# A hybrid decoder layer on one Trainium2 core: weight units of 1024 columns instead of 512

## The chip, the cores and the metric

The kernel runs on one core of one Trainium2 chip. The metric is the device time of one execution in microseconds (us), the lower the better. Of the kernel before there are three timed runs and one profiled execution.

## What is computed

One step of a decoder layer for 1024 new prompt tokens and 32 sample tokens (8 sequences of 4), model width 1024, all in fp32:

```python
proj = x @ w_in                                  # q, k, v, GLA's q, k, v, gates
o_a  = dilated_window_attention(...)             # 3 groups x 8 heads, windows 128, 512, 2048
o_b  = gla_recurrence(...)                       # 4 heads, chunks of 64
x1   = layer_norm(alpha * x + merge(o_a, o_b, gates) @ w_out)
q    = normalise(x1 @ w_peer_query)              # 8 heads
expert, gate = top 16 of 128 x 128 product keys  # per token and head
act  = gelu(x1 . u_table[expert])                # one neuron per expert, 16384 experts
y    = layer_norm(alpha * x1 + sum(gate * act * v_table[expert]))
```

The outputs are y for both groups, the new key and value buffers (for the samples the old ones, shifted) and the new GLA states.

## The kernel before

**fp32 products.** Each fp32 matmul is done as three: operands are split into a high part (a rounded copy, by ScalarE) and a low part (source minus high, by VectorE), and `mm3` (lines 186 to 189) adds high times high, low times high and high times low into one PSUM bank. `split_into` (lines 158 to 160) makes the two parts; the copy is recorded at line 145, in `copy_act`, and the subtraction at line 160.

**Weights.** They are streamed through SBUF. `load_w_` (lines 173 to 184) takes a staging buffer `wst` (three of 2 KB per partition), has SP load 128 x 512 values into it at line 174, takes `wh` and `wl` (four buffers each) and splits. `load_w` calls it at an earlier priority than the code around it. While there are output copies left (old key and value buffers that go from DRAM to DRAM, in the list `copies`), a counter `due` sends one or two of them behind a load, at line 180. All loads, copies and gate reloads are issued by SP, in one order. A staging buffer is free again when VectorE has made the low part from it.

**Stages.** The first 1000 us of the span are projections. From 1000 to 2700 us there are attention, GLA, the merge, the PEER queries and top-k, and gathers begin. From 2700 us on the dense PEER loop runs beside the rest of the gathers. The 1024 prompt tokens are treated in two ways: for one half the experts of each token are gathered (`peer_gather`, line 1217: GpSimd, in the trace POOL, issues one indirect DMA of 128 rows of 1024 values per expert slot, at line 1234 for `pu` and at line 1255 for `pv`; VectorE multiplies and adds up, at lines 1240 and 1273, with four `gr` buffers), for the other half (512 tokens) all 16384 experts are computed densely.

**The dense loop** (`peer_dense`, line 1354) goes over 128 values of e, each standing for 128 experts. For an e there are four pieces of work:

- `hidden(e)`: the uT weights in two units of 512 columns, 24 matmuls into one PSUM bank (`ps<-pg,wh` in the trace), then a gelu on ScalarE at line 1380 into a `t` or `tb` tile;
- `weights(e)`: VectorE multiplies that tile by the gate matrix G (line 1388, two instructions, one for each half of G), then it is split into a pair of `tq`;
- `values(e)`: two loads from `pv` into `wst` at line 1374, split into the two halves of a page `pg`;
- `out`: 18 matmuls for output columns 0 to 5, into PSUM banks that stay open over the whole loop; for each pair of e another 12 for columns 6 and 7, into two `ps` banks that VectorE adds to a sum at line 1423.

`hidden` runs up to seven e ahead. G stands in DRAM; every eight e, line 1407 loads the next eight into two pages (2 transfers of 1 MB). This makes 16 reloads. Pages are one pool of ten, shared by G, the `pv` pairs and the activations of the 512 tokens; the pages for a new G come free when TensorE has done columns 6 and 7 of an earlier pair.

**The order.** A scheduler, which has a simulated timeline of its own, lays the instructions of each engine in one list before the kernel is built. On the chip each engine goes through its list in that order; an instruction that must wait holds up all that is behind it on that engine.

Of the kernel before, what the change touches and what calls it, by code (L numbers as in the profile page):

```python
# [11 lines left out]
F32R = mybir.dt.float32r  # L12
# [9 lines left out]
P = 128  # L22
T = 512
NS = 32
TW = T + NS
D = 1024
# [57 lines left out]
def tile_hybrid_step(ctx, tc, I, O, dbg=None):  # L84
# [31 lines left out]
    def sb(shape, tag, bufs, dt=F32):  # L116
        return sp.tile(list(shape), dt, tag=tag, bufs=bufs, name=nm(tag))
# [5 lines left out]
        return sb(shape, "t2", 8, dt)  # L123

    def tb(shape, dt=F32):
        return sb(shape, "tb", 9, dt)

    def tq(shape, dt=F32):
        return sb(shape, "tq", 6, dt)
# [40 lines left out]
        return r  # L170

    def load_w_(src, shape):
        st = sb(shape, "wst", 3)
        ld = nc.sync.dma_start(st, src)
        due[0] += CRATE
        for _ in range(2):
            if copies and not hush[0] and due[0] >= 1:
                due[0] -= 1
                with tc.issue_after(ld.ins):
                    nc.sync.dma_start(*copies.pop(0))  # L180
        hi = sb(shape, "wh", 4, F32R)
        lo = sb(shape, "wl", 4, F32R)
        split_into(st, hi, lo)
        return hi, lo

# [58 lines left out]
    def tick():  # L244
        for l in lanes.values():
            l[2] += l[1]
            while l[2] >= 1:
                l[2] -= 1
                step(l)
# [249 lines left out]
    def rows_of(toks, src, xs, cols=None, stag=0):  # L499

        outs = [(ps() if i < 4 else (pb if busy[0] else pc)())[:m] for i, m in toks]
        def products(p_, i, m, k, w):
            if i < 4 and cols:
                h, l = [cols(v, i) for v in xs(k, 0, T)]
            else:
                h, l = xs(k, i * P, i * P + m)
            mm3(p_, h, l, *w, k == 0, k == 7)


        for k in range(8):  # L510
            tick()
            if k <= 8 - stag:
                ws = []
            ws.append(load_w(src[:, k], [P, 512]))
            if k < 8 - stag:
                for p_, (i, m) in zip(outs, toks):
                    products(p_, i, m, k, ws[0])
        for p_, (i, m) in zip(outs, toks):
            for j in range(stag):
                products(p_, i, m, 8 - stag + j, ws[j])  # L520
        return outs


    def phase_a(b):
# [18 lines left out]
        def dense_T(src, nk, xs, width=P):  # L543

            out = [(ps(), c0, c1) for (c0, c1) in (segs0 if xs is x else segs)]
            for k0 in range(0, nk, 4):
                wh, wl = load_w(src[:, k0:k0 + 4], [P, 4, width])
                for k in range(k0, k0 + 4):
                    for (p_, c0, c1) in out:
                        h, l = xs(k, c0, c1)  # L550
                        mm3(p_[:width, :c1 - c0], wh[:, k - k0], wl[:, k - k0], h, l, k == 0, k == nk - 1)
            return out

        def proj_T(ci):
# [799 lines left out]
    def peer_dense(x1T, toks):  # L1354
# [4 lines left out]

        def hidden(e):  # L1360
            p_ = ps()
            for k0 in (0, 4):
                wh, wl = load_w(I["uT"][e][:, k0:k0 + 4], [P, 4, P])
                for k in range(4):
                    h, l = x1T(k0 + k, 0, T)
                    mm3(p_, wh[:, k], wl[:, k], h, l, k0 + k == 0, k0 + k == 7)
            return p_

        def values(e):
            v = page([P, 2, D], F32R)  # L1370
            for hf in range(2):
                st = sb([P, 512], "wst", 3)
                c = slice(hf * 512, (hf + 1) * 512)
                nc.sync.dma_start(st, vrows[e][:, c])
                split_into(st, v[:, 0, c], v[:, 1, c])
            return v

        def gelu(e):
# [351 lines left out]
```

## Time and profile before

| what | us |
|---|---|
| timed runs | 4253.96, 4259.05, 4264.85; median 4259.05 |
| profiled execution, its own time | 4250.62 |
| its span, from the first to the last instruction | 4248.5 |
| TensorE busy | 3842.8 (90%) |
| VectorE busy | 3089.3 (73%) |
| ScalarE busy | 1522.4 (36%) |
| GpSimd (POOL) busy | 1324.2 (31%) |

PE is TensorE, DVE VectorE, ACT ScalarE, POOL GpSimd; SP issues DMAs and is not counted as busy. The mean granted clock of TensorE is 0.911 of its full one. Tile names in the profile have no numbers: `ps<-pg,wh` is a matmul into a `ps` bank from an activation page and a high weight part, `wl<-wst,wh` the making of a low part. `A <- B` in a wait means that A waited and that B ended the wait. In the profile 2.1 us of the execution lie outside the span.

### The profile page before, as it was taken

What the parts mean: (1) busy time and instruction counts of PE and PEld (TensorE: products, weight loads), DVE (VectorE), ACT (ScalarE), POOL (GpSimd) and SP (SyncE); (2) the same over time, 40 slices, a digit from 0 to 9 for tenths busy, and PEclk for the clock granted to TensorE, in tenths of its full rate; (3) what the DMA queues carried; (4) which work ended last, traced back from release to release, by engine and by line L of the source; (5) the groups of instructions that cost most, each with busy time, mean ns of one, the idle gap of its engine ahead of it and who ended that gap; (6) DMA issues with size and microseconds to landing.
All of it is one profiled execution on the core that took longest, in us unless ns stands there. A gap on an engine that the chain in (4) does not pass through costs nothing.

```text
span 4248.5 us, 55341 instructions
## 1 busy us (share of the span) xinstructions
PE 3842.8 (90%) x18338; PEld 2908.0 (68%) x18338; DVE 3089.3 (73%) x6887; ACT 1522.4 (36%) x3092; POOL 1324.2 (31%) x1163
## 2 busy tenths in 40 slices
PE   8999999999796789899779977789999999999997
PEld 7898676656685467656667634577777777777776
DVE  2334432548999866688988877898887887888887
ACT  3334222335443344422234447442222233322223
POOL 0000000000345333344544142315444443444441
PEclk9999999999997579779989975799999999999998
DMA  8665565877798778778988466868899898998986
GB/s 270 196 216 191 191 206 169 298 269 247 253 312 278 243 253 277 238 237 293 318 302 277 159 224 236 277 203 288 312 311 313 294 314 300 319 311 303 312 305 217
DMA packets 455158, 1118.36 MB, mean 263 GB/s; under 512 B 48484, under 2 KB 133620, under 8 KB 444486
## 3 DMA queue, kind: packets, MB, share of 16 engines
q0 software_dynamic: 156672, 570.49, 39.4%
q1 hardware_dynamic: 298198, 544.32, 38.6%
q8 instruction: 144, 2.36, 0.2%
q14 instruction: 144, 1.18, 0.1%
HBM read 1044.14 MB, written 158.37 MB: 283 GB/s over the span
## 4 chain that ended last, share of the span: by engine, by line
PE 47%; DMA 16%; issue 14%; DVE 13%; POOL 6%; ACT 4%; SPq 0%; POOLq 0%; DVEq 0%; ACTq 0%
PE ps L187 10%; PE ps L188 10%; PE ps L189 9%; POOL gr L1234 5%; DMA gr<-pv,tkei 5%; DMA pg<-Gd 4%; DMA gr<-pu,tkei 3%; DVE gr L1240 3%; DVE acc L1273 2%; PE pc L1335 1%; DVE wl L160 1%; PE pb L358 1%; DMA wst<-uT 1%; PE pc L1336 1%; POOL gr L1255 1%
## 5 line engine op out<-in xcount | busy, mean ns | idle before, releaser
L187 PE MATMUL ps<-pg,wh 128*128 128x512 f32 (+3 forms) x2488 | 898.9, 363 | 72.3 <-ACT wh L145 52.1
L1255 POOL DMA_INDIRECT gr<-pv,tkei x544 | 662.9, 1219 | 966.3 <-DVE acc L1273 633.8
L1234 POOL DMA_INDIRECT gr<-pu,tkei x544 | 642.3, 1181 | 965.2 <-DVE gr L1240 561.2
L188 PE MATMUL ps<-pg,wl 128*128 128x512 f32 (+3 forms) x2488 | 896.1, 361 | 10.5 <-DVE wl L160 10.5
L189 PE MATMUL ps<-pg,wh 128*128 128x512 f32 (+3 forms) x2488 | 893.9, 360 | 0.0
L145 ACT ACTIVATE wh<-wst 128x512 fp32r<-128x512 f32 x740 | 462.9, 628 | 1183.5 <-DMA wst<-uT 384.4
L160 DVE TENSOR_TENSOR wl<-wst,wh 128x512 fp32r<-128x512 f32 x740 | 502.2, 683 | 375.6 <-ACT wh L145 347.6
L1240 DVE SCALAR_TENSOR_TENSOR gr<-gr,x1g 128x1024 f32<-128x1024 f32 x544 | 659.1, 1218 | 101.3 <-DMA gr<-pu,tkei 99.7
L1273 DVE SCALAR_TENSOR_TENSOR acc<-gr,act,acc 128x1024 f32<-128x1024 f32 x512 | 654.4, 1278 | 82.6 <-DMA gr<-pv,tkei 80.1
L187 PEld LDWEIGHTS ps<-pg,wh 128*128 128x128 f32 (+1 forms) x2488 | 472.9, 190 | 168.4 <-ACT wh L145 57.2
L188 PEld LDWEIGHTS ps<-pg,wl 128*128 128x128 f32 (+1 forms) x2488 | 473.3, 190 | 95.6 <-DVE wl L160 16.7
L189 PEld LDWEIGHTS ps<-pg,wh 128*128 128x128 f32 (+1 forms) x2488 | 472.9, 190 | 77.3 <-issue 10.4
L187 PE MATMUL ps<-wh,pg 128*128 128x512 f32 x832 | 342.2, 417 | 38.3 <-ACT wh L145 18.9
L188 PE MATMUL ps<-wh,pg 128*128 128x512 f32 x832 | 341.0, 410 | 3.6 <-DVE pg L160 3.6
L189 PE MATMUL ps<-wl,pg 128*128 128x512 f32 x832 | 322.3, 414 | 2.1 <-DVE wl L160 1.9
L145 ACT ACTIVATE pg<-wst 128x512 fp32r<-128x512 f32 x256 | 159.8, 630 | 411.6 <-DMA wst<-pv 398.1
L187 PEld LDWEIGHTS ps<-wh,pg 128*128 128x128 f32 x832 | 177.6, 214 | 92.4 <-ACT wh L145 23.8
L187 PE MATMUL ps<-tq,pg 128*128 128x512 f32 x512 | 200.5, 398 | 9.3 <-ACT t L1380 9.3
L188 PEld LDWEIGHTS ps<-wh,pg 128*128 128x128 f32 x832 | 177.8, 214 | 44.0 <-issue 10.2
L1047 POOL MEMSET tq<- 128x512 f32 x6 | 3.1, 524 | 655.4 <-issue 286.8
L189 PEld LDWEIGHTS ps<-wl,pg 128*128 128x128 f32 x832 | 175.1, 213 | 46.1 <-issue 9.8
L188 PE MATMUL ps<-tq,pg 128*128 128x512 f32 x512 | 202.4, 395 | 0.0
(435 smaller groups left out, 6041.1 us busy)
## 6 DMA issues: line engine op xcount, KB each, us to landing
o_old<-cache SPq DMA_DIRECT2D x256, 256.0 KB
wst<-uT SPq DMA_DIRECT2D x256, 256.0 KB
wst<-pv SPq DMA_DIRECT2D x256, 256.0 KB
wst<-wT SPq DMA_DIRECT2D x192, 256.0 KB
Gd<-pg SPq DMA_DIRECT2D x32, 1024.0 KB
pg<-Gd SPq DMA_DIRECT2D x32, 1024.0 KB
wst<-wN SPq DMA_DIRECT2D x112, 256.0 KB
wst<-wq SPq DMA_DIRECT2D x96, 256.0 KB
```

The costliest lines, as they stand in the source:

```text
L145: nc.scalar.activation(out, in_, AF.Copy, scale=scale)
L160: V.tensor_sub(lo, src, hi)
L187: nc.tensor.matmul(out, lh, rh, start=first, stop=False)
L188: nc.tensor.matmul(out, ll, rh, start=False, stop=False)
L189: nc.tensor.matmul(out, lh, rl, start=False, stop=last)
L358: nc.tensor.matmul(p_[r][:, p2, c * P:(c + 1) * P], q[rows, p * P:(p + 1) * P], keys(p, c)[rows], start=True, stop=True)
L1234: nc.gpsimd.indirect_dma_start(out=u, out_offset=None, in_=I["pu"], in_offset=bass.IndirectOffsetOnAxis(ap=ei[:, j:j + 1], axis=0))
L1240: V.scalar_tensor_tensor(u, u, 1.0, x1, ALU.mult, ALU.mult, accum_out=act[:, j:j + 1])
L1255: nc.gpsimd.indirect_dma_start(out=u, out_offset=None, in_=I["pv"], in_offset=bass.IndirectOffsetOnAxis(ap=ei[:, j:j + 1], axis=0))
L1273: V.scalar_tensor_tensor(acc, u, act[:, j:j + 1], acc, ALU.mult, ALU.add, accum_out=None if j < n - 1 or decode else sums[:, 0, 0:1])
L1335: nc.tensor.matmul(p_[:, n4], o1[:, :, n], oh[:, :, n], start=True, stop=False)
L1336: nc.tensor.matmul(p_[:, n4], o1[:, :, n], ol[:, :, n], start=False, stop=True)
```

## The change

A weight unit becomes 1024 columns, 4 KB per partition, loaded by one DMA, with one ScalarE copy and one VectorE subtraction of that width. There are two staging buffers of that size instead of three of half of it, and two `wh` and two `wl` instead of four each; per partition `wst` grows from 6 to 8 KB, and `wh` and `wl` keep 8 KB each. `tb` (2 KB each) has eight buffers instead of nine.

```diff
     def tb(shape, dt=F32):
-        return sb(shape, "tb", 9, dt)
+        return sb(shape, "tb", 8, dt)
...
     def load_w_(src, shape):
-        st = sb(shape, "wst", 3)
+        st = sb(shape, "wst", 2)
         ld = nc.sync.dma_start(st, src)
-        due[0] += CRATE
-        for _ in range(2):
+        due[0] += CRATE * math.prod(shape[1:]) / 512
+        for _ in range(4):
             if copies and not hush[0] and due[0] >= 1:
                 due[0] -= 1
                 with tc.issue_after(ld.ins):
                     nc.sync.dma_start(*copies.pop(0))
-        hi = sb(shape, "wh", 4, F32R)
-        lo = sb(shape, "wl", 4, F32R)
+        hi = sb(shape, "wh", 2, F32R)
+        lo = sb(shape, "wl", 2, F32R)
         split_into(st, hi, lo)
         return hi, lo
...
+        ws = []
         for k in range(8):
             tick()
+            if k % 2 == 0:
+                wh, wl = load_w(src[:, k:k + 2], [P, 2, 512])
             if k <= 8 - stag:
                 ws = []
-            ws.append(load_w(src[:, k], [P, 512]))
+            ws.append((wh[:, k % 2], wl[:, k % 2]))
...
         def dense_T(src, nk, xs, width=P):
 
             out = [(ps(), c0, c1) for (c0, c1) in (segs0 if xs is x else segs)]
-            for k0 in range(0, nk, 4):
-                wh, wl = load_w(src[:, k0:k0 + 4], [P, 4, width])
-                for k in range(k0, k0 + 4):
-                    for (p_, c0, c1) in out:
-                        h, l = xs(k, c0, c1)
-                        mm3(p_[:width, :c1 - c0], wh[:, k - k0], wl[:, k - k0], h, l, k == 0, k == nk - 1)
+            wh, wl = load_w(src, [P, nk, width])
+            for k in range(nk):
+                for (p_, c0, c1) in out:
+                    h, l = xs(k, c0, c1)
+                    mm3(p_[:width, :c1 - c0], wh[:, k], wl[:, k], h, l, k == 0, k == nk - 1)
             return out
...
         def hidden(e):
             p_ = ps()
-            for k0 in (0, 4):
-                wh, wl = load_w(I["uT"][e][:, k0:k0 + 4], [P, 4, P])
-                for k in range(4):
-                    h, l = x1T(k0 + k, 0, T)
-                    mm3(p_, wh[:, k], wl[:, k], h, l, k0 + k == 0, k0 + k == 7)
+            wh, wl = load_w(I["uT"][e], [P, 8, P])
+            for k in range(8):
+                h, l = x1T(k, 0, T)
+                mm3(p_, wh[:, k], wl[:, k], h, l, k == 0, k == 7)
             return p_
 
         def values(e):
             v = page([P, 2, D], F32R)
-            for hf in range(2):
-                st = sb([P, 512], "wst", 3)
-                c = slice(hf * 512, (hf + 1) * 512)
-                nc.sync.dma_start(st, vrows[e][:, c])
-                split_into(st, v[:, 0, c], v[:, 1, c])
+            st = sb([P, D], "wst", 2)
+            nc.sync.dma_start(st, vrows[e])
+            split_into(st, v[:, 0], v[:, 1])
             return v
```

980 units become 490. The weight `wa`, with `nk` = 4, keeps its 16 units of 512 columns, in buffers of which there are now two. Behind the lines that the change shortens, line numbers fall by one or rise by two.

With other units the scheduler lays some instructions in another order. At the reload of G for experts e = 48 to 55, SP's list reads so before:

```order
L174 DMA wst_28621<-uT 128x512
L174 DMA wst_28639<-uT 128x512
L1374 DMA wst_28677<-pv 128x512
L1374 DMA wst_28681<-pv 128x512
L174 DMA wst_28693<-uT 128x512
L1407 DMA pg_28764<-Gd 128x16x128
L1407 DMA pg_28765<-Gd 128x16x128
L174 DMA wst_28711<-uT 128x512
```

and with the change, at the same reload:

```order
L174 DMA wst_26711<-uT 128x1024
L1373 DMA wst_26761<-pv 128x1024
L1406 DMA pg_26838<-Gd 128x16x128
L1406 DMA pg_26839<-Gd 128x16x128
L174 DMA wst_26773<-uT 128x1024
```

The first half of a hidden's uT (`wst_28693`) went ahead of G and the second (`wst_28711`) behind it; now the whole of it (`wst_26773`) is behind G.

ScalarE's list at that place, before (`wh_28713` is split from the half behind G; `tq_28687` is the weight of e = 47, which needs the old G only, `tq_28779` that of e = 48, which needs the new one):

```order
L145 ACTIVATE wh_28641<-wst_28639 128x512
L145 ACTIVATE pg_28676<-wst_28677 128x512
L145 ACTIVATE pg_28676<-wst_28681 128x512
L145 ACTIVATE tq_28687<-tb_28139 128x512
L145 ACTIVATE wh_28695<-wst_28693 128x512
L1380 ACTIVATE tb_28619<-ps_28620 128x512
L145 ACTIVATE tq_28779<-t_5819_28211 128x512
L145 ACTIVATE wh_28713<-wst_28711 128x512
```

and with the change (`tq_26767` is the weight of e = 47, `tq_26849` that of e = 48):

```order
L145 ACTIVATE pg_26760<-wst_26761 128x1024
L145 ACTIVATE wh_26713<-wst_26711 128x1024
L1379 ACTIVATE tb_26569<-ps_26570 128x512
L1379 ACTIVATE t_4971_26631<-ps_26632 128x512
L145 ACTIVATE wh_26775<-wst_26773 128x1024
L145 ACTIVATE tq_26767<-tb_26289 128x512
L145 ACTIVATE tq_26849<-t_4931_26351 128x512
```

The split of the load behind G stood behind both `tq`; now it stands ahead of both.

TensorE's list where it first needs that load, before (the last matmuls of columns 6 and 7 for e = 46 and 47, then the hidden):

```order
L187 MATMUL ps_28748<-tq_28687,pg_28676 128x512
L188 MATMUL ps_28748<-tq_28687,pg_28676 128x512
L189 MATMUL ps_28748<-tq_28688,pg_28676 128x512
L187 MATMUL ps_28692<-pg_19212,wh_28713 128x512
L187 MATMUL pb_22911<-tq_28779,pg_28768 128x512
```

and with the change:

```order
L188 MATMUL ps_26710<-pg_17904,wl_26714 128x512
L189 MATMUL ps_26710<-pg_17906,wh_26713 128x512
L189 MATMUL ps_21475<-tq_26706,pg_26698 128x512
L187 MATMUL ps_26772<-pg_17903,wh_26775 128x512
L188 MATMUL ps_26772<-pg_17903,wl_26776 128x512
```

All the matmuls of e = 47, the first half of the hidden and e = 46's columns 6 and 7 stood ahead of that point; now they stand behind it.

## Rows read from the trace of the kernel before

**Rows 1.** The page, busy us, share of the span and instructions of each engine.

```profile
PE 3842.8 (90%) x18338; PEld 2908.0 (68%) x18338; DVE 3089.3 (73%) x6887; ACT 1522.4 (36%) x3092; POOL 1324.2 (31%) x1163
```

**Rows 2.** Busy time by stretch: us; PE, PEld, DVE, ACT, POOL; granted clock; DMA share; GB/s.

```profile
0.00:1000.00 1000.00, 971.92 (x5838) 729.72 (x5839) 421.93 (x1021) 322.38 (x767) 17.39 (x68) 0.98 0.68 224
1000.00:2700.00 1700.00, 1448.25 (x6518) 1038.54 (x6516) 1399.70 (x3723) 725.05 (x1513) 657.23 (x558) 0.83 0.77 259
3150.00:4249.00 1099.00, 1016.55 (x4285) 815.69 (x4283) 888.11 (x1317) 332.86 (x570) 469.72 (x390) 0.96 0.87 300
```

**Rows 3.** TensorE's waits from 3150 us on: us in total, times, longest.

```profile
PE ps L187 <- ACT wh L145: 48.6, 11, 7.2
PE ps L188 <- DVE wl L160: 6.4, 8, 2.4
```

**Rows 4.** SP's timeline at one reload: start, us.

```profile
3274.24 0.33 SPq L174 DMA_DIRECT2D wst<-uT  x1
3274.61 6.08 SPq L1407 DMA_DIRECT2D pg<-Gd  x2
3280.79 8.44 SPq L174 DMA_DIRECT2D wst<-uT  x1
```

**Rows 5.** SP's waits from 3150 us on.

```profile
SPq L1407 <- PE ps L189: 15.1, 11, 4.2
```

**Rows 6.** VectorE's timeline at that reload: start, us; idle before and its releaser.

```profile
3294.12 0.42 DVE L1388 TENSOR_TENSOR t<-t,pg 128x256 f32<-128x256 f32 x1 [4.81 <-DMA pg<-Gd]
3294.46 0.42 DVE L1388 TENSOR_TENSOR tb<-tb,pg 128x256 f32<-128x256 f32 x1
...
3296.74 1.27 DVE L1273 SCALAR_TENSOR_TENSOR acc<-gr,act,acc 128x1024 f32<-128x1024 f32 x1
3297.94 0.68 DVE L160 TENSOR_TENSOR wl<-wst,wh 128x512 fp32r<-128x512 f32 x1
```

**Rows 7.** The chain of waits from 3100 us on: start, us.

```profile
3275.09 19.00 DMA pg<-Gd
```

**Rows 8.** TensorE's timeline at that reload.

```profile
3284.41 0.39 PE L189 MATMUL pb<-tq,pg 128*128 128x512 f32 x1
...
3290.39 0.39 PE L189 MATMUL ps<-tq,pg 128*128 128x512 f32 x1
3295.78 0.79 PE L187 MATMUL ps<-pg,wh 128*128 128x512 f32 x1 [5.00 <-ACT wh L145]
...
3298.67 0.80 PE L188 MATMUL ps<-pg,wl 128*128 128x512 f32 x1 [0.30 <-DVE wl L160]
```

**Rows 9.** Groups by line from 2700 us on: busy, mean ns of one, idle before.

```profile
L160 DVE TENSOR_TENSOR wl<-wst,wh 128x512 fp32r<-128x512 f32 x240 | 163.5, 685 | 32.5 <-ACT wh L145 32.3
L145 ACT ACTIVATE pg<-wst 128x512 fp32r<-128x512 f32 x254 | 158.6, 630 | 408.5 <-DMA wst<-pv 398.1 <-PE ps L189 4.9 <-DVE pg L929 4.6
```

**Rows 10.** The tile `acc`: shortest, median and longest ns of one, when.

```profile
L145 ACT ACTIVATE acc<-x1g x5: 1042/1059/1357, 940.4 to 3551.4; 128x1024 f32<-128x1024 f32 x4, 32x1024 f32<-32x1024 f32 x1
L967 DVE TENSOR_TENSOR acc<-acc,gr x5: 1208/1225/1226, 1879.0 to 4208.2; 128x1024 f32<-128x1024 f32 x4, 32x1024 f32<-32x1024 f32 x1
```

**Rows 11.** The page, DMA queues: packets, MB, share of 16 engines (q0 gathers, q1 SP).

```profile
q0 software_dynamic: 156672, 570.49, 39.4%
q1 hardware_dynamic: 298198, 544.32, 38.6%
```

**Rows 12.** ScalarE's timeline at the start.

```profile
10.75 0.63 ACT L145 ACTIVATE wh<-wst 128x512 fp32r<-128x512 f32 x1 [0.57 <-DMA wst<-wN]
12.03 0.63 ACT L145 ACTIVATE wh<-wst 128x512 fp32r<-128x512 f32 x1 [0.65 <-DMA wst<-wN]
```

**Rows 13.** Groups by line, 1000 to 2700 us: attention's transposes.

```profile
L384 PE MATMUL pb<-c_ident,tb 128*128 128x128 f32 x192 | 43.3, 343 | 38.8 <-ACT tb L377 38.8
```

**Rows 14.** The page, costliest groups: the two gather issues.

```profile
L1255 POOL DMA_INDIRECT gr<-pv,tkei x544 | 662.9, 1219 | 966.3 <-DVE acc L1273 633.8
L1234 POOL DMA_INDIRECT gr<-pu,tkei x544 | 642.3, 1181 | 965.2 <-DVE gr L1240 561.2
```

## The prediction, made before the changed kernel ran

> **What bounds the kernel now.** I read the page's busy times first [rows 1]: TensorE works for 90% of the span, VectorE for 73%, ScalarE for 36%. An average says little, so the table by stretches came next [rows 2]. In the first 1000 us TensorE is busy for 972, which leaves weights little to hold up. From 1000 to 2700 us, with gathers and attention, 252 us of TensorE's time are idle. From 3150 us on, where the dense PEER loop runs alone with the gathers, it is busy for 1017 of 1099 us, so 82 are idle. The waits of that last stretch [rows 3] name who ends them: 48.6 us in 11 waits for a high part `wh`, 6.4 us in 8 waits for a low part `wl`. Eleven is the number of G reloads there, one for every eight experts; the stretch thus has one kind of stall.
>
> One such stall, the reload for experts 48 to 55, can be followed. SP issues half of a uT unit, then the two transfers of G, then the next uT half [rows 4]. SP's waits show what holds G back: the matmuls that free its two pages [rows 5], those of the outputs 6 and 7 of an earlier expert pair. G is issued at 3274.61; VectorE can use its second half at 3294.12 [rows 6], 19.5 us later, and from 3100 us on the chain of waits runs through this transfer at eight reloads, 19.0 us at this one [rows 7]. Meanwhile TensorE lives on what needs neither G nor a weight that is queued behind G. It runs until 3290.8, stands 5.0 us until the next `wh`, and meets the `wl` at 3298.67 [rows 8]. From the 27 rows between 3284.41 and 3290.39 one matmul takes 5.98 / 26 = 0.230 us. In ScalarE's order that `wh` comes behind the `tq` that needs G. VectorE, after G's second half, multiplies six tiles, splits one `tq`, does one gather's accumulation and only then the `wl` [rows 6]. So the stall is not a matter of split speed: its length is G's flight plus some 4.6 us, minus the matmuls that are left over.
>
> **The change, part by part.** 980 units of 256 KB become 490 of 512 KB; 490 splits on ScalarE, 490 on VectorE and 490 transfers on SP go.
>
> *Wider splits.* A 512-wide split takes 0.630 us on ScalarE and 0.685 on VectorE [rows 9]; the nearest 1024-wide ones take 1.059 and 1.225 [rows 10]. Per pair that saves 2 x 0.630 - 1.059 = 0.20 and 2 x 0.685 - 1.225 = 0.15 us; over 490 units 98 us of ScalarE and 71 of VectorE. In the first stretch and in the dense loop nothing waits for it apart from the reloads, so I cost it at nothing there: TensorE's own work covers it, and without that cover it would be a part of those 71 us. The dense loop holds 494 of the 996 splits [rows 9], so 36 of VectorE's 71 us; of the other 35, the stretch from 1000 to 2700 us holds about 1700 / 2700, 22 us. VectorE is busy there for 1400 of 1700 us [rows 2], so most of that goes into its slack: **-4**, with bounds -22 and 0.
>
> *The reload.* This is the main term, and it comes from the order, not from durations. Count the matmuls in TensorE's order from the last one that frees G's pages to the first one that needs a `wl` of a uT unit loaded behind G. In the twelve reloads from expert 32 on, the kernel before has 62 to 84 there, 71 on average. With the change there are 42 to 48, 45 on average. Three things cost the 26: the half unit that could go ahead of G no longer exists; in eight of the twelve ScalarE now has the blocked `wh` in front of the `tq` of the expert before, which needs no new G; and a hidden is now 24 matmuls in one piece, so that expert's matmuls mostly stand behind the blocked one anyhow. When the restart comes is little changed: five multiplications (5 x 0.34), one accumulation (1.20), one addition (0.68, as a split of that size) [rows 6] and the wide `wl` (1.22) behind G's second half make 4.8 us; before, it was 3298.67 - 3294.12 = 4.6. So each of the twelve stalls grows by 26 x 0.230 = 6.0 us. Against that, the uT half of 256 KB that used to fly with G's 2 MB is out of its way: at most 0.25 / 2.25 x 19.0 = 2.1 us, of which I take 1.0, since the whole units ahead of G may still be in flight. 12 x 5.0 = **+60**; bounds 12 x 3.9 = 47, and, as at some reloads two more additions and a `tq` split stand in front of the `wl` on VectorE, 12 x 8.0 = 96.
>
> In the last two reloads TensorE's order has two matmuls of the parked `tq` after only 18, ahead of a hidden that could run. TensorE restarts there once that `tq` is split, some 3 us behind G, but with 27 matmuls (6.2 us) still to do where the others wait for the `wl` at 4.8: 3 + 6.2 - 4.8 = 4.4 us each, **+9**, bounds 0 and 9. Reloads 1 to 3 lose 0, 10 and 6 matmuls by the count: 16 x 0.230 = **+4**, bounds 0 and 8. The time lost isn't given back later, for between reloads TensorE has no idle time that work ahead could fill.
>
> *Longer transfers.* A 4 KB packet per partition in place of 2 KB: the queue whose packets average 544.32 MB / 298198 = 1.8 KB costs 38.6 / 544.32 = 0.0709% of the engines' time per MB, the one with 3.6 KB packets 0.0691% [rows 11]. That is 2.5% less per byte, and no wait hangs on it: 0. The Trainium skill, "Perfetto Trace Analysis", section "DMA Optimizations", says that batching transfers from 2 KB to 4 or 8 KB can improve throughput dramatically. Were the weights' half of that queue's bytes to cost half by it, about 9% of the engines' time would be free, G would land some 1.7 us sooner, and as an estimate the sum would be 20 us smaller; the two packet sizes of this trace speak against it.
>
> *Start.* TensorE's first matmul needs the first unit. The second half's split begins at 12.03 us, the first one's at 10.75 [rows 12]; a whole unit needs both loads and a longer split, 1.28 + 0.43 = **+1.7**, bounds 0 and 3.
>
> *Smaller pools.* The 16 units of `wa` stay 512 wide but have two staging buffers instead of three, and `tb` has eight buffers instead of nine. No row prices this; the nearest is attention's wait for `tb`, 38.8 us over 192 transposes [rows 13]. An eighth of it is **+5**; bounds 0 and 25. The output copies that follow a load come three in a row instead of one or two; they ride behind loads in a stretch where TensorE waits for 28 us of 1000 in all: 0.
>
> Sum: 60 + 9 + 4 + 1.7 + 5 - 4 = +76 on the profiled execution's 4250.6, so 4326. The median of the three runs is 8.4 above that execution, which gives **4335 us**. The bounds add up to 4259 + 47 - 22 = 4284 and 4259 + 96 + 9 + 8 + 3 + 25 = 4400.
>
> **The rivals.** About 0.3%, 13 us, is what a measurement of this kernel can tell from no change.
>
> *Faster: G lands early, and the gather stage pays out.* If fewer transfers were in flight beside G, it would land sooner. For the stall to stay as it is, it has to land 6.0 us sooner, in 13 us instead of 19; at the 300 GB/s of that stretch [rows 2] its 2 MB alone need 7, so there is room. Against it: the gathers remain, and they hold 39.4% of the engines [rows 11]. Should the VectorE time of the gather stage be on the path as well, the end is 4259 - 22 - 20 (of ScalarE's 0.20 us a unit there, some 29 us, two thirds) + 2 = 4219. The point that decides is G's flight under 13 us. 0.15.
>
> *No change.* G lands in about 13 us but the gather stage hides its gain, or ScalarE's order costs less since the `tq` behind the `wh` is not what TensorE wants first: 4259 + 5 = 4264. The twelve terms would have to vanish almost whole, or half of them and the gather stage give its 22 us. 0.10.
>
> *Slower by the gathers.* Beside the reload, weight packets that take about twice as long (0.088 us each now: 0.386 x 16 x 4248.5 / 298198 [rows 11]) delay each gather packet behind them. A gather fetches 128 rows of 4 KB, 8 per engine, so 8 x 0.088 = 0.7 us more; if a quarter of that shows, because gathers overlap, the 1088 gathers [rows 14] take 1088 x 0.17 = 185 us longer, half of it in the dense loop. Against it, POOL waits 634 and 561 us for VectorE [rows 14], which is slack. With half of the reload's cost: 4259 + 92 + 34 = 4385. The Trainium skill, "DMA: Bandwidth & Descriptors", section "Queues, rings and completion order", states that an engine alternates between queue rows a whole packet at a time, which is this mechanism; no run here has yet shown what it costs. 0.08.
>
> **How the numbers follow.** The forecast, the reload's term, has 0.67. It and the gathers make slower 0.75; no change 0.10; faster 0.15. The forecast's own range is 4284 to 4400. The whole range goes from 4245, the edge of faster, which leaves out the 0.15, to 4395, which leaves out the forecast's upper end and a part of the gathers' case.
>
> **What would show it.** In the changed profile, from 3150 us on: TensorE's waits for `wh` and `wl` at the reloads grow from 55 us to about 115 in as many waits, each of 8 to 13 us; their idle time, not their busy time, carries the difference; G's flight stays at 17 to 19 us; the distance between reloads goes from 97 to about 102 us. The first 1000 us keep their pace within 5 us. ScalarE's splits are about 1.06 us, VectorE's 1.22. Wrong would be: stalls of 5 us as before (then G came sooner, or the order isn't what starves TensorE), a first stretch that is over 10 us longer (pools, copies), or gathers that POOL waits for by DMA.

## The result, and the profile after

The median is 4291.68 us (six runs, 4279.29 to 4297.85) against 4260.75 for the kernel before on the same chip: a ratio of 1.0067 [1.0045, 1.0088], 31 us slower. The forecast of 4335 had the sign and, with its range, the time; it had 76 us for the 31, and most of all it had them in the wrong place.

The page's busy times answer to [rows 1]:

```profile
PE 3843.2 (90%) x18338; PEld 2910.6 (68%) x18338; DVE 3052.6 (71%) x6397; ACT 1430.3 (33%) x2600; POOL 1439.3 (34%) x1163
```

VectorE lost 37 us and ScalarE 92. The page counts the time of overlapping instructions once; added up one by one, the splits take 74 us less on VectorE and 99 less on ScalarE, and 71 and 98 were expected. TensorE's busy time is the same to 0.4 us, so the loss is waiting. Where? By stretch, as in [rows 2] (us; PE, PEld, DVE, ACT, POOL; granted clock, DMA share, GB/s):

```profile
0.00:1000.00 1000.00, 963.11 (x5739) 723.80 (x5740) 391.25 (x857) 290.11 (x639) 17.97 (x68) 0.97 0.63 218
1000.00:2700.00 1700.00, 1422.42 (x6380) 1022.88 (x6379) 1352.16 (x3517) 651.07 (x1312) 680.66 (x539) 0.83 0.74 252
3150.00:4278.00 1128.00, 1069.65 (x4594) 862.09 (x4592) 934.64 (x1232) 315.76 (x418) 550.78 (x416) 0.98 0.88 310
```

The last stretch is *better* than before: 58 us idle of 1128, where it was 82 of 1099. Up to 2700 us TensorE did 237 matmuls fewer than before. Cutting by time hides where one kernel falls behind, so the better cut is one event that both have: SP's first issue of G, which opens the dense PEER loop. Before, it is at 2698.21, after at 2776.37 (SP's timeline of each):

```profile
2698.21 2.91 SPq L1407 DMA_DIRECT2D pg<-Gd  x2
```

```profile
2776.37 3.33 SPq L1406 DMA_DIRECT2D pg<-Gd  x2
```

The two sides of that event, by stretch, first of the kernel before:

```profile
2698.00:4248.50 1550.50, 1422.60 (x5984) 1139.73 (x5984) 1269.60 (x2153) 476.11 (x814) 649.57 (x537) 0.96 0.86 293
0.00:2698.10 2698.10, 2420.17 (x12354) 1768.26 (x12354) 1819.81 (x4737) 1046.28 (x2278) 674.61 (x626) 0.88 0.74 246
```

then of the changed kernel:

```profile
2776.40:4278.40 1502.00, 1400.98 (x5984) 1129.14 (x5984) 1256.48 (x1917) 428.86 (x566) 717.86 (x537) 0.97 0.87 302
0.00:2776.30 2776.30, 2442.24 (x12354) 1781.48 (x12354) 1796.04 (x4481) 1001.43 (x2034) 721.42 (x626) 0.87 0.70 239
```

The count of matmuls is the same in both, 5984 and 12354, so the pieces compare directly. **The dense part became 48 us shorter** (27 less idle, 22 less busy), **and what lies ahead of it 78 us longer** (56 more idle, 22 more busy). 78 - 48 = 30 is the difference of the two profiled spans. The lag of TensorE's n-th matmul, taken from both traces, grows in steps: 9 us at 800 us of the kernel before, 22 at 1045, 36 at 1789, 82 at 2286; then it falls to 30 at the end. The weight `wa` is passed twice, once for each half of the tokens. The first passage ends within the step up to 1045, the second lies within the largest step, the 46 us from 1789 to 2286.

**The dense part.** TensorE's waits from 3150 us on answer to [rows 3]:

```profile
PE ps L187 <- DVE tb L1422: 28.4, 21, 4.4
PE pb L187 <- ACT tq L145: 6.0, 5, 3.9
PE ps L187 <- ACT t L1379: 5.0, 3, 2.3
```

The 48.6 us for `wh` and the 6.4 for `wl` are gone; 39 us of shorter waits of other kinds stand in their place (8 us before). The reload of experts 48 to 55 shows why. SP, as in [rows 4]; its waits that the view puts down to the pages, as in [rows 5]; and two of its waits from 3310 to 3325 us:

```profile
3318.78 0.33 SPq L174 DMA_DIRECT2D wst<-uT  x1
3321.90 0.33 SPq L1373 DMA_DIRECT2D wst<-pv  x1
3322.28 5.41 SPq L1406 DMA_DIRECT2D pg<-Gd  x2
3330.12 6.27 SPq L174 DMA_DIRECT2D wst<-uT  x1
```

```profile
SPq L1406 <- PE ps L189: 43.5, 9, 6.9
```

```profile
SPq L1406 <- PE ps L189: 4.0, 1, 4.0
SPq L1373 <- DVE pg L160: 2.7, 1, 2.7
```

TensorE there, as in [rows 8], with the hidden that needs the load behind G at 3349.53:

```profile
3320.28 0.39 PE L189 MATMUL ps<-tq,pg 128*128 128x512 f32 x1
...
3335.11 0.39 PE L187 MATMUL ps<-tq,pg 128*128 128x512 f32 x1
...
3338.97 0.39 PE L189 MATMUL ps<-tq,pg 128*128 128x512 f32 x1
...
3343.63 0.50 PE L187 MATMUL ps<-pg,wh 128*128 128x512 f32 x1 [0.42 <-DVE tb L1422]
...
3349.31 0.39 PE L189 MATMUL ps<-tq,pg 128*128 128x512 f32 x1
3349.53 0.40 PE L187 MATMUL ps<-pg,wh 128*128 128x512 f32 x1
```

G's pages come from columns 6 and 7 of the pair *before* the one that I counted from: those matmuls end at 3320, and G leaves at 3322.28. The pair that I took, e-4 and e-3, does its columns only from 3335.11 to 3338.97. So the pages are free when SP gets to G. It leaves right behind a `pv` load that had waited 2.7 us for its staging buffer, until VectorE was done with it. At all twelve reloads from expert 32 on it is so: the first transfer of G waits for no matmul, and the load ahead of it waits for VectorE, 1.9 to 2.7 us at eleven of them.

The nine waits for a matmul that the view names fall into the second transfer's issue, which takes 4.8 to 5.5 us where none is named, too; the matmul is each time one of a hidden, which frees no page of G. In the kernel before, the first transfer stood for a freeing matmul, but at most 0.46 us, behind loads that waited 0.2 to 2.1 us for a staging buffer; 13.9 of the 15.1 us of [rows 5] lie in the second transfer's issue.

VectorE and ScalarE, as in [rows 6]:

```profile
3336.69 0.42 DVE L1387 TENSOR_TENSOR t<-t,pg 128x256 f32<-128x256 f32 x1 [1.02 <-DMA pg<-Gd]
...
3340.02 0.43 DVE L1387 TENSOR_TENSOR t<-t,pg 128x256 f32<-128x256 f32 x1 [0.37 <-DMA pg<-Gd]
...
3344.56 1.22 DVE L160 TENSOR_TENSOR wl<-wst,wh 128x1024 fp32r<-128x1024 f32 x1 [0.98 <-ACT wh L145]
```

```profile
3343.47 1.06 ACT L145 ACTIVATE wh<-wst 128x1024 fp32r<-128x1024 f32 x1 [10.32 <-DMA wst<-uT]
```

From its issue to VectorE's first use of its second half G took 17.7 us, as long as forecast. The `wl` begins 4.5 us behind that and is ready 5.8 us behind it, at 3345.78, where 4.8 was forecast; it waited for its `wh`, and that for its own load from behind G. But TensorE has 27 us of work from G's issue on, until 3349.53, and never meets it. Take the matmuls from the issue of G's second transfer to the first one that needs a `wh` loaded behind G, over the twelve reloads from expert 32 on: TensorE has 53 to 74 of them left in the kernel before (64 on average) and 91 to 127 in the changed one (115). The distance between reloads went from 97.2 to 93.2 us.

Groups from 2700 us on, as in [rows 9]; the queues, as in [rows 11]; attention's wait for `tb`, as in [rows 13]; the start, as in [rows 12]; the gather issues, as in [rows 14]:

```profile
L160 DVE TENSOR_TENSOR wl<-wst,wh 128x1024 fp32r<-128x1024 f32 x120 | 146.2, 1219 | 4.5 <-ACT wh L145 4.4
L145 ACT ACTIVATE wh<-wst 128x1024 fp32r<-128x1024 f32 x120 | 126.7, 1056 | 395.8 <-DMA wst<-uT 309.0 <-PE ps L189 60.8 <-DVE t L1387 12.1
```

```profile
q0 software_dynamic: 156672, 570.49, 38.6%
q1 hardware_dynamic: 227638, 544.29, 37.1%
```

```profile
L384 PE MATMUL pb<-c_ident,tb 128*128 128x128 f32 x192 | 43.0, 344 | 39.0 <-ACT tb L377 39.0
```

```profile
11.07 1.06 ACT L145 ACTIVATE wh<-wst 128x1024 fp32r<-128x1024 f32 x1 [0.97 <-DMA wst<-wN]
```

```profile
L1257 POOL DMA_INDIRECT gr<-pv,tkei x544 | 710.8, 1307 | 927.6 <-DVE acc L1275 558.3
L1236 POOL DMA_INDIRECT gr<-pu,tkei x544 | 708.9, 1303 | 901.8 <-DVE gr L1242 467.8
```

### The profile page after: what moved, and what is told of

It reads as the page before. It is cut to its first block, busy times and chain, and to the rows that moved or that the text cites. A ratio compares the mean times of both kernels' runs of the same rounds, so it can differ in the third digit from the quotient of the medians.

```text
span 4278.4 us, 52718 instructions
## 1 busy us (share of the span) xinstructions
PE 3843.2 (90%) x18338; PEld 2910.6 (68%) x18338; DVE 3052.6 (71%) x6397; ACT 1430.3 (33%) x2600; POOL 1439.3 (34%) x1163
## 3 DMA queue, kind: packets, MB, share of 16 engines
q1 hardware_dynamic: 227638, 544.29, 37.1%
## 4 chain that ended last, share of the span: by engine, by line
issue 15%; DMA 13%; POOL 10%; PE 6%; DVE 5%; ACT 2%; POOLq 0%; DVEq 0%; ACTq 0%
DMA gr<-pv,tkei 11%; POOL gr L1236 6%; POOL gr L1257 4%; DMA gr<-pu,tkei 1%; DVE acc L1275 1%; ACT tb L1325 1%; PE ps L187 1%; PE ps L189 1%; PE ps L188 1%; PE pb L1337 1%; PE pb L1338 1%; DVE gr L1242 1%; DVE pg L160 0%; PE pc L1269 0%; DVE wl L160 0%
## 5 line engine op out<-in xcount | busy, mean ns | idle before, releaser
L1257 POOL DMA_INDIRECT gr<-pv,tkei x544 | 710.8, 1307 | 927.6 <-DVE acc L1275 558.3
L1236 POOL DMA_INDIRECT gr<-pu,tkei x544 | 708.9, 1303 | 901.8 <-DVE gr L1242 467.8
L145 ACT ACTIVATE wh<-wst 128x1024 fp32r<-128x1024 f32 (+1 forms) x378 | 390.7, 1034 | 958.6 <-DMA wst<-uT 314.2
L160 DVE TENSOR_TENSOR wl<-wst,wh 128x1024 fp32r<-128x1024 f32 (+1 forms) x378 | 450.3, 1192 | 263.3 <-ACT wh L145 253.4
L145 ACT ACTIVATE pg<-wst 128x1024 fp32r<-128x1024 f32 x128 | 136.1, 1063 | 445.7 <-DMA wst<-pv 435.2
```

The lines of the kernel that those rows point to most:

```text
L145: nc.scalar.activation(out, in_, AF.Copy, scale=scale)
L160: V.tensor_sub(lo, src, hi)
L1236: nc.gpsimd.indirect_dma_start(out=u, out_offset=None, in_=I["pu"], in_offset=bass.IndirectOffsetOnAxis(ap=ei[:, j:j + 1], axis=0))
L1257: nc.gpsimd.indirect_dma_start(out=u, out_offset=None, in_=I["pv"], in_offset=bass.IndirectOffsetOnAxis(ap=ei[:, j:j + 1], axis=0))
```

## The experiments

Two questions: what takes 78 us ahead of the dense part, and what gave 48 in it? Every kernel is read by the same two numbers, the first G's issue and the time from there to the end of the span (the dense part); the last column counts matmuls as above. Times are medians, ratios are against the kernel before in the same series (4254 to 4258 in the experiments). The other columns come from one profiled execution of each kernel: hold44, which leaves the dense loop alone, has 1515 us for the changed kernel's 1502, so a difference of some 13 us between two of them says little.

| kernel | us | ratio to before | first G | dense part | matmuls left at G |
|---|---|---|---|---|---|
| before | 4260.75 | | 2698.2 | 1550 | 64 |
| after | 4291.68 | 1.0067 [1.0045, 1.0088] | 2776.4 | 1502 | 115 |
| hold44 | 4291.55 | 1.0069 [1.0053, 1.0085] | 2776.7 | 1515 | 115 |
| proj_half | 4286.59 | 1.0063 [1.0047, 1.0079] | 2760.7 | 1521 | 117 |
| dense_half | 4303.85 | 1.0089 [1.0072, 1.0106] | 2779.2 | 1523 | 115 |
| before_tb8 | 4298.81 | 1.0087 [1.0065, 1.0109] | 2727.1 | 1572 | 67 |
| after_tb9 | 4291.54 | 1.0090 [1.0074, 1.0106] | 2758.7 | 1526 | 116 |
| before_early80 | 4285.55 | 1.0069 [1.0054, 1.0084] | 2732.9 | 1558 | 66 |
| before_tb10 | 4274.80 | 1.0041 [1.0026, 1.0057] | 2716.0 | 1548 | 73 |
| wa2 | 4272.80 | 1.0045 [1.0029, 1.0061] | 2743.4 | 1525 | 115 |
| wa2_tb9 | 4266.23 | 1.0024 [1.0009, 1.0039] | 2737.3 | 1535 | 116 |
| after_early80 | 4293.10 | 1.0083 [1.0060, 1.0106] | 2771 | 1519 | 116 |
| wa2_tb9_e130 | 4262.27 | 1.0011 [0.9996, 1.0026] | 2737.4 | 1523 | 115 |
| wa2_tb9_e80 | 4258.62 | 1.0013 [1.0001, 1.0025] | 2740 | 1519 | 115 |
| before_wst4 | 4229.53 | 0.9940 [0.9919, 0.9961] | 2714.2 | 1515 | 125 |
| before_wst4_e80 | 4210.14 | 0.9892 [0.9869, 0.9915] | 2698.1 | 1520 | 122 |

**hold44.** In the changed kernel the last 44 steps of the generator that issues gathers are held back until the output projection of the second half is done.

```
+HOLD = 44
...
-            advance(gen, P + turn[0])
+            advance(gen, P + turn[0] - HOLD)
...
+                with tc.issue_after(merged[-1].ins):
+                    advance(gen, 1)
+                advance(gen, HOLD - 1)
```

> The changed kernel, but the last 44 of the gathers that the scheduler may lay where it likes are held back until the output projection of the second half is done; VectorE's order then has 414 gathers ahead of the end of that stage, as the kernel before has 415, where the changed kernel has 441. Theory A (the gathers' place: in the stage of attention, GLA and merge every gather costs about 2.57 us of the path, in the query stage behind it none): the 27 gathers that move back give 27 x 2.57 = 69 us at most and some 45 at least, so 4225 to 4250 us, below the kernel before, since the dense loop keeps its gain of 50. Theory B (the wide units and their two staging buffers slow that stage themselves): 4280 to 4300, as the changed kernel.

Between the matmuls that bound the largest step of the lag (1825 to 2367 us in the changed kernel) there were 189 gathers instead of 205. The stretch lasted 534 us instead of 543, but the first G stayed at 2776.7 and the time at 4291.55. Where the gathers lie is not the cause: the first theory fell.

**proj_half and dense_half.** The changed kernel's pools, with weights loaded and split in two pieces of 512 columns (`t` is a half of the buffer, `s` its source) into one buffer of 1024: once the projections' weights, once those of the dense loop.

```
+        st, parts = sb([P, n], "wst", 2), []
...
+            ld = nc.sync.dma_start(t if len(s.shape) == 2 else t.rearrange("p (a b) -> p a b", a=s.shape[1]), s)
...
+            split_into(t, hi[:, c], lo[:, c])
```

> The projections load and split in pieces of 512 columns again, two DMAs and two splits into the halves of the same two buffers of 1024; the dense loop keeps whole units. VectorE's order has 426 gathers ahead of the end of the merge stage (before 415, changed 441). Theory A: 15 gathers fewer than the changed kernel at 2.57 us, so about 39 us less: 4253, with 4240 to 4265. Theory B (wide pieces slow the projections): nearly all of the 80 us ahead of the dense loop come back, 4210 to 4225. If the pieces matter in neither way: 4292.

Neither outcome: the dense part stays short as with whole units, and of the 78 us ahead of it 62 remain.

> The projections keep whole units; hidden and values load and split in pieces of 512 columns again, two DMAs and two splits into the halves of the same buffers. The order of gathers up to the dense loop is that of the changed kernel (441). Theory C (the dense loop's gain of 50 us comes from whole units, through the time at which G is issued): the gain goes, 4335 to 4345, with stalls of about 5 us on the high part at each reload. Theory D (it comes from the two larger staging buffers or from fewer gathers, not from whole units): 4285 to 4300.

Mixed, and the more telling. The splits in the dense loop are those of before again, yet G still leaves with 115 matmuls of work left. TensorE's waits from 3150 us on:

```profile
PE ps L210 <- DVE tb L1447: 33.9, 21, 8.0
PE pb L210 <- ACT tq L145: 15.1, 9, 3.7
PE ps L210 <- ACT t L1404: 1.9, 1, 1.9
```

The waits for `wh` don't come back, but for one of 0.9 us. So the gain in the dense part doesn't hang on a wide operation; it came with the pools. The width itself is worth little there: this dense part is 21 us longer than the changed kernel's, but only 2.5 longer than that of proj_half, whose dense loop is wide.

**before_tb8 and after_tb9.** The ninth buffer of `tb`, taken from the kernel before, and given back to the changed one (smaller `tke`, `gate` and `tkei` pay for its 2 KB).

```
-        return sb(shape, "tb", 9, dt)
+        return sb(shape, "tb", 8, dt)
```

> The kernel before with eight tb buffers instead of nine and nothing else. VectorE's order has 424 gathers ahead of the end of the merge stage instead of 415. Theory A: 9 x 2.57 = 23 us more, 4275 to 4290, all of it ahead of the dense loop. If only the buffer itself counts, as the prediction had it: 0 to 5 us more, 4260 to 4266.

> The changed kernel with nine tb buffers again. The 2 KB come from three small pools (tke 4 to 2 buffers, gate 5 to 4, tkei 5 to 4), which in the kernel before leave every engine's order as it was. Theory E (the lost tb buffer is what the changed kernel pays: the kernel before lost 41 us by it alone): 4292 - 41 = 4251, with 4240 to 4262. Theory F (no single buffer counts; the order of the kernel before is a favourable one, and whatever makes the scheduler lay the instructions anew costs 20 to 45 us): 4275 to 4300.

Taken away it costs 41 us; given back it returns nothing. And of the 50 us between the profiled spans, 21 arise in the dense part (1571.7 for 1550.3). TensorE's longest item of waits from 3150 us on is of the old kind, 13 waits instead of 11:

```profile
PE ps L187 <- ACT wh L145: 43.6, 13, 6.0
```

A buffer whose loss costs 41 us in one kernel and whose return gives none in the other is hardly short in itself. What both edits also do is make the scheduler lay out another order.

**before_early80 and before_tb10.** So the next two change the order of the kernel before without making anything scarcer: once by the number by which a weight load is put ahead in the scheduler's priorities, once by one buffer *more*.

```
-EARLY = 100
+EARLY = 80
```

> The kernel before with one number of the scheduler changed, the priority by which weight loads are drawn forward: 80 instead of 100. All buffers, loads, splits and matmuls are as before; only the order differs (as much as with eight tb buffers: some 60% of VectorE's rows stand in the same sequence). Theory E: 4250 to 4266, no change. Theory F: 4275 to 4300.

> The kernel before with ten tb buffers instead of nine, the 2 KB from the same three small pools. One buffer more can't make anything wait longer for a buffer. Theory E: 4235 to 4262, a gain or no change. Theory F: 4275 to 4300, a loss like that of one buffer less.

31 us slower by a number that removes no resource, 20 us slower with a buffer more (1.0069 and 1.0041, neither interval near 1). The order of the kernel before is a favourable one beside these three, and an edit that disturbs it can pay for that. So a part of the change's loss need be no property of wide units; how large a part isn't shown. Nor is that order the only good one: before_wst4_e80, below, opens its dense part as early (2698.1).

**wa2, wa2_tb9 and after_early80.** In the changed kernel `wa` alone kept 512-column units, each of which takes one of only two staging buffers of 1024. wa2 loads it in pairs.

```
+            if c % 2 == 0:
+                w2 = load_w(I["wa"][c:c + 2].rearrange("c p k n -> p c k n"), [P, 2, 4, P])
```

> The changed kernel with wa loaded in pairs of its 512-column pieces, so that its 16 units too become 8 of 1024 columns; before, each of them held one of the only two buffers of wst, wh and wl half empty. Theory G (wa with two half-used buffers costs the changed kernel some 15 us in each of the two merges, 171 and 195 us from the first wa load to the first wq load where the kernel before takes 156 and 172): both go back to about 156 and 175, and the total to 4292 - 35 = 4257, with 4245 to 4270. Theory F (whatever order the scheduler lays, the kernel lies 20 to 45 us above the one before): 4275 to 4300.

> The same with nine tb buffers (2 KB from the three small pools). Theory G: as with eight, 4240 to 4270, since nine buffers by themselves gave the changed kernel nothing. Theory F: 4275 to 4300.

> The changed kernel with the scheduler's priority for weight loads at 80 instead of 100, the change of order that cost the kernel before 31 us. Theory F (the kernel before has a favourable order, and the changed kernel already has an ordinary one): 4275 to 4310, no loss like that. If a new order costs any kernel some 30 us: 4310 to 4330.

wa2 brings the first G from 2776 to 2743. Of these 33 us 23 go again in the dense part (1525 for 1502), and the ratios, 1.0067 and 1.0045, have intervals that overlap; with the ninth `tb` as well, 1.0024 lies clear of the change's. SP's loads in the second half show it at the place itself. In the changed kernel the eight units begin at 2061.68, and `wq` follows at 2256.64, 195 us on:

```profile
2061.68 0.33 SPq L174 DMA_DIRECT2D wst<-wa  x1
2078.89 0.33 SPq L174 DMA_DIRECT2D wst<-wa  x1
2125.96 2.77 SPq L174 DMA_DIRECT2D wst<-wa  x2
...
2256.64 0.33 SPq L174 DMA_DIRECT2D wst<-wq  x1
```

With `wa` in pairs it is 180 us:

```profile
2048.43 0.38 SPq L174 DMA_DIRECT2D wst<-wa  x1
...
2228.93 0.33 SPq L174 DMA_DIRECT2D wst<-wq  x1
```

Before the change it is 172 (2012.84 to 2184.92). So 15 us came back there. In the first half the same passage took 156 us before the change, 171 with it and 176 with `wa` in pairs, so 5 were lost again: 10 of the 33 us can be pointed at, and the other 23 aren't located. That `wa` in pairs opens the dense part earlier does not hang on one order: the four kernels with it open at 2737 to 2743, the six other kernels with the changed pools at 2759 to 2779. A new order in the changed kernel (after_early80) costs nothing beyond scatter: its order was an ordinary one already, as the reading of the last pair wants it.

**wa2_tb9_e130 and wa2_tb9_e80** are two more orders of the repaired change, to see how much of its distance to the kernel before an order can make up.

> Wide units, wa in pairs and nine tb buffers, with the scheduler's priority for weight loads at 130 instead of 100: another order of the best variant so far (4266). If orders scatter by some 12 us about their mean, as those of the kernel before with one number or buffer changed do (4275, 4286, 4299), this lies between 4245 and 4285; below 4246 it would beat the kernel before. If 4266 is what wide units give in whatever order: 4260 to 4272.

> The same with 80 in place of 100, the change that cost the kernel before 31 us and the changed kernel nothing. Scatter: 4245 to 4285. No scatter with wide units: 4260 to 4272. As in the kernel before (+31): 4290 to 4300.

4262.27 and 4258.62 against 4253.59: with `wa` repaired and an order tried or two, wide units come to about 0.1% of the kernel before, and not ahead of it, though their dense parts are 27 and 31 us shorter (1523 and 1519).

**before_wst4 and before_wst4_e80.** If the pools made the dense part shorter, the old units should have it too with as many bytes of staging: four buffers of 512 columns, 8 KB per partition as the change has it, where the kernel before had three (the same smaller `tke`, `gate` and `tkei` pay).

```
-        st = sb(shape, "wst", 3)
+        st = sb(shape, "wst", 4)
...
-            e = sb([P, nh, 16], "tke", 4)
+            e = sb([P, nh, 16], "tke", 2)
-        gate = sb([P, nh, 16], "gate", 5)
+        gate = sb([P, nh, 16], "gate", 4)
-        ei = sb([P, 16 * nh], "tkei", 5, I32)
+        ei = sb([P, 16 * nh], "tkei", 4, I32)
```

> The kernel before, units of 512 columns, with four staging buffers wst instead of three (the 2 KB from the three small pools), so as many bytes of staging as the changed kernel. Theory H (the dense loop's gain of the changed kernel comes from the bytes that can be staged: SP is no longer held at a full wst and reaches G earlier): about 115 matmuls are left when G is issued instead of 64, the reloads' distance is 93 to 95 us instead of 96 to 97, and the dense part takes some 1520 us instead of 1550. Theory I (it comes from wh and wl in pairs, which lets ScalarE and VectorE split a whole hidden at once, or from the order of the pages): 64 left, 1545 to 1570. The total stays open by the order: 4225 to 4285 by H, 4255 to 4300 by I.

> The same in another order, the scheduler's priority for weight loads at 80 instead of 100. By H 115 matmuls left again, by I 64; in total within 20 us of the other.

Shown: 125 matmuls are left at G, TensorE's waits for `wh` are gone, and the dense part takes 1515 us. Its waits from 3150 us on, and its dense part:

```profile
PE ps L187 <- ACT t L1380: 27.4, 8, 5.8
PE ps L187 <- DVE tb L1423: 15.1, 11, 4.3
```

```profile
2714.20:4228.80 1514.60, 1411.24 (x5984) 1139.02 (x5984) 1270.06 (x2155) 464.59 (x814) 660.29 (x537) 0.96 0.87 300
```

0.9940 [0.9919, 0.9961]; with another order also 0.9892 [0.9869, 0.9915], 4210.14 us. Both beat both kernels, without a single wide unit. The smaller `tke`, `gate` and `tkei` don't do it: before_tb10 has them too, and keeps 73 matmuls and 1548 us. The gain of the change in the dense part is the fourth 2 KB of staging, with which SP gets to G sooner: all twelve kernels with 8 KB of it have 115 to 125 matmuls left and dense parts of 1502 to 1535 us, the four with 6 KB 64 to 73 and 1548 to 1572. The Trainium skill, "Perfetto Trace Analysis", section "Optimization Strategy", says that the same gap recurring on the engine that should be full can mean that the next tile finds no memory, by buffer count or tile size. [Rows 3] showed such a gap, eleven times, and the two runs agree: with one more buffer it is gone.

## Why the prediction was right and wrong

**The reload (+60, and +13 beside it): wrong, sign included.** The step that failed is "Count the matmuls in TensorE's order from the last one that frees G's pages to the first one that needs a `wl` of a uT unit loaded behind G", with its "with the change 42 to 48, 45 on average". For the kernel before, 71 was right: counted to the `wl`, as that step does, the trace has 69, and to the `wh` 64. For the changed one I started the count at the same pair, e-4 and e-3, and took for granted that its columns 6 and 7 free G's pages there as well, and that G leaves when they do. Neither holds: the pages come from a pair earlier, G leaves when the load ahead of it has got its staging buffer, and 115 matmuls are left (to the `wl` 117, for my 45). The reading behind it, that the matmuls hold G back, was already loose for the kernel before, where G's first transfer stood 0.46 us for them at most.

The other half of that step came near in size. G's flight was 17.7 us at the reload shown and 19.7 by the median of the twelve (18.4 in the kernel before), and the whole `wl` was ready 5.8 us behind it for 4.8, by another way: it waited for a load and not for VectorE's work on G. At 0.230 us, 64 and 115 matmuls are 14.7 and 26.5 us, against 17.7 + 4.5 + 1.2, and say what was seen: a stall before, none after. The stalls being gone, the +9 and the +4 for the other reloads are nothing as well. Why the scheduler gives G the pages of an earlier pair wasn't tried by itself; that more staging brings it about is shown by before_wst4.

**Ahead of the dense part (+5 for pools, +1.7, -4): mis-sized, +78.** The runs point at three things. A favourable order that was lost: the kernel before, with its three staging buffers and a number or a `tb` buffer changed, opens the dense part 18 to 35 us later. `wa` in half-filled staging buffers: 10 us shown in place, 33 by wa2's first G. And a rest that stays open, about 10 us by the larger figures and 50 by the smaller ones. One of the signs of being wrong that I had named came with it: the first 1000 us were to keep their pace within 5 us, and TensorE was 22 us behind at 1045, with 16 us of that in the first passage of `wa`. Two of my reasons for +5 can be checked by rows. The wait for `tb` is 39.0 us where it was 38.8, so one buffer less did not work by that wait; `wa` did, and its price, 10 to 33 us, lies around my bound of 25 for both pools together. That a new order has a price of its own was no term at all.

**Wider splits.** Right in size: 1.056 and 1.219 us for 1.059 and 1.225. That they give nothing on the path in the dense loop is not refuted: dense_half is 2.5 to 21 us longer there than kernels with wide splits, order and scatter included.

**Transfers.** 0 was right. The packets of SP's queue went from 298198 to 227638, and its share per MB from 0.0709% to 37.1 / 544.29 = 0.0682%; with the spans, that is 3% less time per byte. The rule that was weighed there, of the Trainium skill's "Perfetto Trace Analysis", section "DMA Optimizations" (batching from 2 KB to 4 or 8 can improve throughput dramatically), would by the estimate made from it have brought 20 us; for these sizes the trace disagrees.

**Start.** The first split begins at 11.07 and ends at 12.13 where it ended at 11.38: 0.75 us instead of 1.7.

**The rivals.** *Faster, G lands early*: from its first issue G's flight did not fall to 13 us (17.2 at the least); the stall went by another way. *The gathers*: the median flight of a gather in the dense part is 6.80 us after 6.62 before, +0.18, about the size that this rival gave. From 3150 us on VectorE waits 122 us for gathers where it was 61, but no wait of TensorE there names a gather, and POOL still waits 558 and 468 us for VectorE. That the longer flight costs no time is argued by these rows, not shown by a run. *"Idle time, not busy time, carries the difference"* was wrong in part, which is the last section.

Right in sign, then, but by luck: the loss came from terms that I had at 5 us, while the term that carried the forecast turned out a gain.

## What to carry to other kernels

When a loop stalls at a reload, try one more staging buffer before a wider unit: here the bytes gave the gain (0.6%, and 1.1% with another order), the width little of it, and a wide pool charges every narrow tenant a whole slot. Read what releases a transfer from the changed kernel's own order, as it need not be the same there, and look at each wait that a view names: one that falls into the transfer's own issue may be no wait. And where a scheduler lays out the order, time two or three neutral neighbours of a tuned kernel before an edit is blamed or credited: here they alone cost 0.4 to 0.7%.

## What was not expected of the hardware

A stall cost more than its idle time. At the reload of [rows 8] the kernel before has, around the 5.0 us in which TensorE stands (columns as in [rows 2]):

```profile
3284.40:3290.80 6.40, 6.38 (x28) 4.88 (x26) 2.10 (x6) 0.00 (x0) 0.35 (x1) 1.00 1.07 368
3295.80:3298.60 2.80, 2.57 (x5) 1.43 (x5) 2.80 (x6) 0.97 (x2) 0.31 (x1) 0.50 0.00 0
3298.70:3301.00 2.30, 2.30 (x7) 1.89 (x8) 2.30 (x4) 0.00 (x0) 1.64 (x2) 0.70 0.53 165
3302.00:3308.00 6.00, 6.00 (x28) 4.92 (x27) 6.00 (x10) 2.38 (x4) 4.21 (x3) 1.00 0.96 335
```

The granted clock is 1.00, 2.4 GHz, up to the stall, 0.50, 1.2 GHz, behind it, and 1.00 again from 3302 on; the first matmul behind the stall takes 0.79 us where the last one ahead of it took 0.39 [rows 8]. The 12 matmuls of the two middle rows are busy for 4.87 us, 2.1 more than 12 x 0.230. Eleven such stalls would make 23 us, as an estimate from this one, and the dense part's busy time fell by 22 (1422.60 to 1400.98) when they went. Between 3150 and 4200 us the granted clock fell to 0.50 eleven times in the kernel before and four times in the changed one. My price of 0.230 us for a lost matmul left that out.

POOL's gather issues take 1.30 us on average in the changed kernel where they took 1.18 and 1.22 [rows 14], at the same median of 1.14. It goes with the wide loads: 1.18 to 1.24 in the six kernels that have none, 1.25 to 1.33 in the ten others. Nothing shows the reason, and the kernel has no wait of TensorE for POOL in the dense part.
